# Second token half loaded into the tile of its low part, and a larger planned price for a transfer on SyncE

## The chip, the cores and the metric

The kernel runs on one core of a Trainium2 chip. Time is the device time of one execution in microseconds (us). Besides the plain runs there is one profiled execution, whose trace gives the start and the end of every instruction. The engines are named as in the profile: PE (TensorE matmul; PEld is its weight load), DVE (VectorE), ACT (ScalarE), POOL (GpSimd), SP (SyncE, which here only issues DMA transfers; its queue is "SPq").

## The reference

One decoder layer on x of 1024 tokens by 2048 channels, all in float32:

```python
h = rmsnorm(x, ln_g)
proj = h @ w_in                       # 2048 -> 6672 columns
g_u, g_v, g_z, d_q, d_k, d_v, d_z, d_a, d_b, c_q, c_z = split(proj)
out_a = gmlp_spatial_gating(g_u, g_v, ...) * silu(g_z)      # 4 groups of 128, chunks of 128 tokens
q, k, v = heads(causal_conv_silu(concat(d_q, d_k, d_v)))    # 8 heads of 128
o = gated_delta_rule(l2norm(q), l2norm(k), v, g, beta)      # chunks of 64: a 64x64 triangular
out_b = rmsnorm(o, dn_norm_g) * silu(d_z)                   # solve, then a scan of the state
out_c = cross_attention(c_q, mem) * silu(c_z)               # 4 heads, 256 memory tokens
y = rmsnorm(x + concat(out_a, out_b, out_c) @ w_out, final_g)
```

## The kernel before, in words

**Products.** A float32 product is made of three matmuls on parts: `split_to(hi, lo, src, eng)` (line 422) lets ACT copy `src`, rounded, into `hi` (in the profile a CAST), and DVE subtract, `lo = src - hi` (a TENSOR_TENSOR). A triple on PE is then hi·hi + lo·hi + hi·lo, each 128x128 by 128x512, accumulated in a PSUM bank `acc`. `ahi[k]`, `alo[k]` are the parts of the normalised tokens, transposed: 16 tiles k of 128 channels by 512 tokens. `whi`, `wlo` are the parts of the weights.

**Two token halves.** The 1024 tokens go in two halves of 512. `ahi`/`alo` hold one half at a time, 128x512 float32 per k (256 KB). While the first half is projected, the second one is normalised and its 16 transposed tiles are written to DRAM, `hT_d`, as are those of the first, `h0_d`. When the first half is done, `refill(k)` (lines 1218 to 1223) brings tile k of the second half from `hT_d[k]` into `ahi[k]`, `alo[k]`, with k running inside the first product that uses it: `project([column(0, 0), column(1, 0)], before)` (line 1232) makes two columns of 128 at once, for each k first `refill(k)`, then a small matmul for the decays, then two triples (6 large matmuls).

**The raw ring.** `wraw` (lines 372 to 380) is a ring of four slots of 128x512. Weight pieces are loaded into it (`raw_piece`, line 426) and split from there into `whi`, `wlo`. In the kernel before, `refill` takes its slots from the same ring. The ring hands its slots out in the order of the program's text, so a load waits until the slot's previous content has been split.

**What follows a refill.** Gated DeltaNet for pairs of heads: `front` (columns, convolution), `inverted` (the triangular inverse: 31 dependent steps of small DVE operations), `values`, and `back` with `scan_step` (PE products `dn<-...`; `vs`, `states`, `steps` are its tiles). `left_sums(j)` (line 725) runs beside it: it loads four tiles (`hTd`, `h0d`) into `zg`, forms sums and differences and stores them to `s_d`; these serve a later, Strassen-like stage that works on both halves at once (loads `raws<-sd`, `y<-sd`, to about 1440 us), before the output product and the final norm. `vd` and `od` in DRAM keep what the scans hand on.

**What sets the order.** Nothing is issued as the text stands. Every operation is recorded as an `Op`, and `Plan.issue` (lines 218 to 277) sorts them all with a small model of the chip: each engine is free at some time, each operation has a `cost` (and a transfer also a data time at `DMA_RATE` 300 bytes/ns and a fixed 1600 ns), a result is seen on another engine some 35 to 78 ns later, PE gets 600 ns more (`SLACK`). The engine that can go first takes the ready operation of the lowest rank (`with rank(n)`); the list, sorted by the planned time, is then emitted, and line 277, `o.fn(*o.args, **o.kw)`, is the line of every instruction in the profile. `Plan.price` (line 180) sets the costs; for a `dma_start` on SP it is 380 ns before. Per engine the emitted order is fixed; the chip runs it with waits on semaphores, so SP issues its transfers strictly in that order, and one whose tile isn't free yet holds all behind it.

Of the kernel before, what the change touches and what calls it, by code (L numbers as in the profile page):

```python
# [9 lines left out]
F32 = mybir.dt.float32  # L10
# [52 lines left out]
class Plan:  # L63
# [21 lines left out]
    @contextmanager  # L85
    def rank(self, cls):
        old, self.cls = self.cls, cls
        yield
        self.cls = old
# [91 lines left out]
    def price(self, o, name, outs, ins):  # L181

        out = outs[0]
        n = math.prod(out.shape[1:])
        both = [*outs, *ins]
        psum = any(i.space == PSUM for i in both)
        pointer = any(i.shape[-1] == 1 and math.prod(i.shape[1:]) == 1 for i in ins[1:])
        o.nbytes = o.lock = 0
        o.lat = 0.0
        if name == "dma_start":  # L190
            o.cost = {"sp": 380.0, "act": 100.0, "pool": 800.0}[o.eng]
            rows = math.prod(out.shape[:-1])
            o.nbytes = max(4 * math.prod(out.shape), 512 * rows)
            src = ins[0]
            pieces = src.shape[-1] < 128 or out.shape[-1] < 128
            if out.space == DRAM:
                o.lat = 3000.0
            elif pieces or out.shape[0] < 32:
                o.lat = 2400.0
            elif list(src.ap)[0][0] == 0:  # L200
                o.lat = 4000.0
        elif o.eng == "pe":
            passes = 1 if ins[0].dtype == F32R else 2 if name == "transpose" else 4
            o.cost = max(13.3 + n / 2.4 * passes, 222.0 if passes == 4 else 110.0) if out.shape[0] == P else 30.0
            o.lat = 175.0
        elif o.eng == "act":
            o.cost = (165.0 if psum else 200.0) + 0.82 * n + (105.0 if pointer else 0.0)
            o.cost += 190.0 if "accum_out" in o.kw else 0.0
        elif o.eng == "dve":
            n = max([n] + [math.prod(i.shape[1:]) for i in ins])  # L210
            o.cost = (n + 151) / 0.96 + (60.0 if pointer and name == "scalar_tensor_tensor" else 0.0)
            o.lock = not psum and (name.startswith("tensor_") or name == "scalar_tensor_tensor")
            o.lock = o.lock and name != "tensor_reduce"
        else:
            o.lock = 1
            if name in ("memset", "affine_select"):
                o.cost = 100.0 + 0.83 * n * (1 if name == "memset" else 1.4)
                o.lat = 800.0 if name == "affine_select" else 0.0
            else:
                o.cost = 750.0 + 150.0 * (n - 1) if n < 8 else 200.0 + 2.1 * n  # L220
# [60 lines left out]
def kernel(  # L281
# [29 lines left out]
    V, S, G, PE, Q = R.dve, R.act, R.pool, R.pe, R.sp  # L311
# [5 lines left out]
    def DT(shape, name, dt=F32):  # L317
        return dr.tile(list(shape), dt, name=name, tag=name)[:]
# [41 lines left out]
    def tok(ap):  # L360

        return ap.rearrange("p (t c) -> p t c", c=P)
# [7 lines left out]
    ahi = [ahq[k // 4][:, :, k % 4] for k in range(KT)]  # L370
    alo = [alq[k // 4][:, :, k % 4] for k in range(KT)]
    wraw = Ring("wraw", 2, [P, 2 * HT])
# [33 lines left out]
    hT_d = DT([KT, P, HT], "hTd")  # L406
# [15 lines left out]
    def split_to(hi, lo, src, eng):  # L422
        S.copy(hi, src)
        eng.tensor_tensor(out=lo, in0=src, in1=hi, op=ALU.subtract)
# [145 lines left out]
    for k in range(KT):  # L570
# [5 lines left out]
        with rank(2):  # L576
            for sl in kv_parts(k):
                raw = kvraw[k % 4][:, sl]
# [638 lines left out]

    def refill(k):

        raw = wraw()  # L1220
        with rank(2):
            Q.dma_start(raw, hT_d[k])
            split_to(ahi[k], alo[k], tok(raw), V)

    a = tpb()

    def before(k):
        refill(k)
        decay_mm(a, k)
# [555 lines left out]
```

## Time and profile before

| | before |
|---|---|
| median of 3 runs | 1644.65 us (1640.99 to 1645.63) |
| profiled execution | 1644.06 us, span 1642.3 us |
| PE busy | 1615.6 us (98%), 8570 matmuls |
| DVE busy | 1317.5 us (80%) |
| ACT busy | 1023.9 us (62%) |
| mean DMA rate | 255 GB/s, 419.51 MB |
| granted PE clock | 0.996 |

The busy rows say how long an engine worked anywhere in the span. For an engine that is 98% busy the question is where the other 2% are, and that is read from the time line and from the waits, not from the shares.

### The profile page before, as it was taken

How to read it: one execution, taken by the hardware profiler on the slowest of the kernel's cores; microseconds unless marked ns; L12 is line 12 of the kernel's file. 1: busy time of each engine (PE TensorE's matmuls, PEld its weight loads, DVE VectorE, ACT ScalarE, POOL GpSimd, SP SyncE). 2: the span in 40 equal slices, each digit the busy share in tenths (PEclk: the TensorE clock that was granted, in tenths of full speed). 3: DMA queues.
4: the chain of work that ended last, by engine and by line, in shares of the span. 5: the costliest groups of instructions: out<-in, count | busy, mean ns of one | idle time of the engine just before them, and what ended most of it. 6: DMA issues, size and time to landing. Idle time of an engine off the chain costs nothing.

```text
span 1642.3 us, 26178 instructions
## 1 busy us (share of the span) xinstructions
PE 1615.6 (98%) x8570; PEld 1354.3 (82%) x8570; DVE 1317.5 (80%) x2288; ACT 1023.9 (62%) x2235; POOL 109.8 (7%) x139
## 2 busy tenths in 40 slices
PE   8999999999999999999999999999999999999997
PEld 6888887878788888888888887888888888888886
DVE  4866796847879869899998997788768897688875
ACT  6957674665855457976776446766666774344445
POOL 0001100120210001100101000000000000000001
PEclk9999999999999999999999999999999999999999
DMA  8889887885886867689878986878968769678646
GB/s 266 255 229 283 256 272 209 249 266 177 278 290 221 267 219 254 207 276 323 298 243 263 304 240 188 297 253 300 313 218 286 260 231 353 202 264 304 219 142 242
DMA packets 316659, 419.51 MB, mean 255 GB/s; under 512 B 57773, under 2 KB 138342, under 8 KB 316522
## 3 DMA queue, kind: packets, MB, share of 16 engines
q1 hardware_dynamic: 314818, 414.67, 77.6%
q0 software_dynamic: 1088, 2.10, 0.4%
q8 instruction: 67, 1.10, 0.3%
q10 hardware_dynamic: 616, 1.07, 0.2%
q14 instruction: 70, 0.57, 0.1%
HBM read 334.33 MB, written 82.87 MB: 254 GB/s over the span
## 4 chain that ended last, share of the span: by engine, by line
PE 89%; DMA 4%; DVE 3%; ACT 1%; issue 1%; SPq 1%; POOLq 0%; POOL 0%; DVEq 0%; ACTq 0%
PE acc L277 68%; PE dn L277 21%; DMA raws<-sd 1%; DMA wraw<-in_w_in_dram 1%; SPq L277 1%; DVE alo L277 1%; DVE wlo L277 0%; DMA od<-vs 0%; DVE y L277 0%; DMA zg<-h0d 0%; ACT whi L277 0%; DMA wraw<-in_w_out_dram 0%; DMA h0d<-tn 0%; DMA el<-vd 0%; DMA y<-in_w_out_dram 0%
## 5 line engine op out<-in xcount | busy, mean ns | idle before, releaser
L277 PE MATMUL acc<-ahi,whi 128*128 128x512 f32 (+1 forms) x1152 | 450.8, 392 | 4.1 <-ACT whi L277 2.1
L277 PE MATMUL acc<-alo,whi 128*128 128x512 f32 (+1 forms) x1152 | 451.7, 392 | 0.2 <-DVE alo L277 0.2
L277 PE MATMUL acc<-ahi,wlo 128*128 128x512 f32 (+1 forms) x1152 | 450.2, 391 | 0.4 <-DVE small L277 0.4
L277 PEld LDWEIGHTS acc<-ahi,whi 128*128 128x128 f32 x1152 | 216.9, 188 | 46.4 <-ACT whi L277 2.7
L277 PEld LDWEIGHTS acc<-ahi,wlo 128*128 128x128 f32 x1152 | 217.0, 188 | 41.7 <-DVE wlo L277 0.6
L277 PEld LDWEIGHTS acc<-alo,whi 128*128 128x128 f32 x1152 | 217.0, 188 | 41.2 <-DVE alo L277 0.9
L277 PE MATMUL acc<-ahi,zh 128*128 128x512 f32 x736 | 233.0, 393 | 0.0
L277 ACT CAST whi<-wraw 128x512 fp32r<-128x512 f32 (+1 forms) x170 | 137.1, 808 | 113.1 <-PE acc L277 73.2
L277 DVE TENSOR_TENSOR alo<-raws,ahi 128x1024 fp32r<-128x1024 f32 x131 | 159.8, 1221 | 39.8 <-ACT ahi L277 38.8
L277 ACT CAST ahi<-raws 128x1024 fp32r<-128x1024 f32 x131 | 137.4, 1049 | 68.8 <-PE dn L277 28.1
L277 DVE TENSOR_TENSOR wlo<-wraw,whi 128x1024 fp32r<-128x1024 f32 (+1 forms) x138 | 135.1, 980 | 49.0 <-ACT whi L277 39.2
L277 PEld LDWEIGHTS acc<-ahi,zh 128*128 128x128 f32 x736 | 137.0, 188 | 26.9
L277 PE MATMUL acc<-ahi,zl 128*128 128x512 f32 x368 | 145.0, 394 | 0.0
L277 DVE TENSOR_TENSOR ahi<-y,ahi 128x1024 fp32r<-128x1024 f32 x65 | 79.4, 1222 | 18.6 <-ACT ahi L277 18.3
L277 ACT CAST ahi<-y 128x1024 fp32r<-128x1024 f32 x65 | 68.3, 1051 | 35.0 <-PE acc L277 18.6
L277 PEld LDWEIGHTS acc<-ahi,zl 128*128 128x128 f32 x368 | 69.3, 188 | 13.4
L277 ACT CAST zh<-wraw 128x1024 fp32r<-128x1024 f32 x36 | 37.8, 1051 | 51.8 <-issue 23.2
L277 POOL TENSOR_TENSOR small<-small,mhalf 128x1 f32<-128x1 f32 x26 | 17.9, 692 | 626.9 <-DVE small L277 626.9
L277 PE MATMUL dn<-wlo,ahi 128*128 128x512 f32 x152 | 59.0, 389 | 0.0
L277 PE MATMUL dn<-whi,alo 128*128 128x512 f32 x152 | 59.0, 389 | 0.0
L277 POOL TENSOR_TENSOR hs<-hs,mhalf 128x4 f32<-128x4 f32 x32 | 46.7, 1460 | 182.7 <-DVE hs L277 181.7
L277 PE MATMUL dn<-whi,ahi 128*128 128x512 f32 x152 | 58.8, 389 | 0.0
(408 smaller groups left out, 3205.3 us busy)
## 6 DMA issues: line engine op xcount, KB each, us to landing
wraw<-in_w_in_dram SPq DMA_DIRECT2D x268, 256.0 KB
raws<-sd SPq DMA_DIRECT2D x148, 256.0 KB
y<-in_w_in_dram SPq DMA_DIRECT2D x92, 256.0 KB
y<-sd SPq DMA_DIRECT2D x77, 256.0 KB
wraw<-in_w_out_dram SPq DMA_DIRECT2D x64, 256.0 KB
raws<-h0d SPq DMA_DIRECT2D x54, 256.0 KB
y<-in_w_out_dram SPq DMA_DIRECT2D x33, 256.0 KB
low<-wlo SPq DMA_DIRECT2D x32, 256.0 KB
```

Source lines behind the costliest of these rows:

```text
L277: o.fn(*o.args, **o.kw)
```

## The change

Two edits. `Plan.price` prices a transfer issued on SP at 490 ns instead of 380 ns. And `refill(k)` no longer takes a slot of `wraw`: it loads `hT_d[k]` into `alo[k]` itself, seen as plain float32, in the tile's own layout (`tok` turns the 128x512 source into 128x4x128; a row of `alo[k]` is four pieces of 128 floats that lie 4x128 floats apart); the split then reads that tile, writes `ahi[k]`, and subtracts in place, `alo[k] = alo[k] - ahi[k]`.

```diff
@@ -188,7 +188,7 @@
         if name == "dma_start":
-            o.cost = {"sp": 380.0, "act": 100.0, "pool": 800.0}[o.eng]
+            o.cost = {"sp": 490.0, "act": 100.0, "pool": 800.0}[o.eng]
@@ -1217,10 +1217,10 @@
     def refill(k):
 
-        raw = wraw()
+        raw = alo[k].bitcast(F32)
         with rank(2):
-            Q.dma_start(raw, hT_d[k])
-            split_to(ahi[k], alo[k], tok(raw), V)
+            Q.dma_start(raw, tok(hT_d[k]))
+            split_to(ahi[k], alo[k], raw, V)
```

Both edits change what the planner counts with, and so the emitted order. On PE the first 461 of 6733 rows of the order (equal neighbours make one row) and the last 853 are the same before and after; on SP, of 1456 rows, the first 64 and the last 62. In between, rows stand earlier or later by a few to some tens of places. Three places follow, of SP and of PE (in a row: operation, out<-in with the number of each tile's allocation, shape).

**SP at the refills, before:** the last 11 of the 16 loads `wraw<-hTd` lie between weight pieces (`in_w_in_dram`), all in the same ring.

```order
L277 DMA wraw1_72<-hTd_114 128x512
L277 DMA wraw0_71<-hTd_114 128x512
L277 DMA wraw0_71<-in_w_in_dram 128x4x128
L277 DMA zg0_81<-h0d_113 128x512
L277 DMA wraw1_72<-hTd_114 128x512 x2
L277 DMA wraw0_71<-in_w_in_dram 128x4x128
L277 DMA wraw0_71<-hTd_114 128x512
L277 DMA wraw1_72<-in_w_in_dram 128x4x128 x2
L277 DMA wraw0_71<-hTd_114 128x512 x2
L277 DMA wraw1_72<-hTd_114 128x512 x2
L277 DMA wraw0_71<-hTd_114 128x512
L277 DMA wraw0_71<-in_w_in_dram 128x4x128
```

**SP at the refills, after:** tiles 5 to 15, into `alo1` to `alo3` (each name is a block of four k).

```order
L277 DMA alo1_68<-hTd_114 128x4x128
L277 DMA wraw0_71<-in_w_in_dram 128x4x128
L277 DMA alo1_68<-hTd_114 128x4x128 x2
L277 DMA sd0_1_3_307<-zg0_81 128x512
L277 DMA alo1_68<-hTd_114 128x4x128
L277 DMA alo2_69<-hTd_114 128x4x128
L277 DMA zg0_81<-h0d_113 128x512
L277 DMA alo2_69<-hTd_114 128x4x128 x3
L277 DMA alo3_70<-hTd_114 128x4x128 x3
L277 DMA wraw1_72<-in_w_in_dram 128x4x128
L277 DMA alo3_70<-hTd_114 128x4x128
L277 DMA wraw1_72<-in_w_in_dram 128x4x128
```

Between the fifth and the last refill there stood four weight pieces, now there are two; the others went behind, and the last refill load is eight rows earlier in SP's order.

**SP at a left sum, before:** `gt` is filled for the next inverse; behind it stand `E`, a low part, and then the two `zg` loads of `left_sums`.

```order
L277 DMA gt_6_452<-gt_6_452 64x4x64
L277 DMA E0_83<-gcd1_371 128x4x128
L277 DMA wlo0_75<-low2944_2_420 128x512
L277 DMA zg1_82<-hTd_114 128x512
L277 DMA wraw1_72<-in_w_in_dram 128x4x128
L277 DMA zg0_81<-h0d_113 128x512
L277 DMA wlo1_76<-low2944_3_421 128x512
```

**After:**

```order
L277 DMA gt_6_452<-gt_6_452 64x4x64
L277 DMA zg1_82<-hTd_114 128x512
L277 DMA zg0_81<-h0d_113 128x512
L277 DMA wlo1_76<-low2944_3_421 128x512
L277 DMA wraw1_72<-in_w_in_dram 128x4x128
L277 DMA E0_83<-gcd1_371 128x4x128
L277 DMA wlo1_76<-low3840_0_443 128x512
```

The two `zg` loads follow `gt` directly. On PE, in the same place, **before** one large matmul of the next column stands ahead of the four `steps` products of the scan and six behind them, up to `dn<-states,kT`:

```order
L277 MATMUL acc0_105<-ahi0_63,whi4_77 128x512
L277 MATMUL dn0_109<-steps_367,kd_6_407 128x128
L277 MATMUL dn1_110<-steps_367,kd_7_422 128x128
L277 MATMUL dn0_109<-steps_367,ai_6_411 128x128
L277 MATMUL dn1_110<-steps_367,ai_7_426 128x128
L277 MATMUL acc0_105<-alo0_67,whi4_77 128x512
```

**after** 13 of them stand ahead:

```order
L277 MATMUL acc0_105<-alo0_67,whi4_77 128x512
L277 MATMUL acc0_105<-ahi0_63,wlo4_78 128x512
L277 MATMUL acc0_105<-ahi1_64,whi0_73 128x512
L277 MATMUL dn0_109<-steps_367,kd_6_407 128x128
L277 MATMUL dn1_110<-steps_367,kd_7_422 128x128
L277 MATMUL dn0_109<-steps_367,ai_6_411 128x128
L277 MATMUL dn1_110<-steps_367,ai_7_426 128x128
L277 MATMUL acc0_105<-alo1_68,whi0_73 128x512
```

so that the scan's products stand 12 large matmuls later in the column's run.

**SP at `el`, before:** a tile that PE reads for the late scan comes behind four stores `vd`, a `gt`, two loads and a load `xd`.

```order
L277 DMA vd1_0_264<-E1_84 128x128
L277 DMA vd1_1_265<-E1_84 128x128
L277 DMA vd1_2_266<-E1_84 128x128
L277 DMA vd1_3_267<-E1_84 128x128
L277 DMA gt_15_627<-gt_15_627 64x4x64
L277 DMA raws_498<-sd0_4_3_319 128x512
L277 DMA raws_498<-sd0_5_3_323 128x512
L277 DMA xd00_0_244<-y2_501 128x512
L277 DMA el0_517<-vd0_2_262 128x512
L277 DMA xd00_1_245<-y2_501 128x512
L277 DMA tn3_88<-vd0_3_263 128x512
```

**After:** `xd00_0` and `el0` stand ahead of the four `vd`; the second pair, `xd00_1` and `tn3`, still behind them.

```order
L277 DMA xd00_0_244<-y2_501 128x512
L277 DMA el0_517<-vd0_2_262 128x512
L277 DMA vd1_0_264<-E1_84 128x128
L277 DMA vd1_1_265<-E1_84 128x128
L277 DMA vd1_2_266<-E1_84 128x128
L277 DMA vd1_3_267<-E1_84 128x128
L277 DMA xd00_1_245<-y2_501 128x512
L277 DMA tn3_88<-vd0_3_263 128x512
```

Elsewhere: the stores `od0_2<-vs`, `od0_3<-vs` of a scan, which before stood right behind four loads `raws<-h0d`, stand after the change behind ten more transfers (`y3` twice two, `raws` four, `wraw1` two).

## The prediction

> **What bounds the kernel now.** I read the page first, for who is busy and what ends last.
>
> ```profile
> span 1642.3 us, 26178 instructions
> PE 1615.6 (98%) x8570; PEld 1354.3 (82%) x8570; DVE 1317.5 (80%) x2288; ACT 1023.9 (62%) x2235; POOL 109.8 (7%) x139
> PE 89%; DMA 4%; DVE 3%; ACT 1%; issue 1%; SPq 1%; POOLq 0%; POOL 0%; DVEq 0%; ACTq 0%
> ```
>
> PE bounds it, and the change gives PE nothing less to do: the count of matmuls stays. So the time can only move by PE's idle time, 1642.3 - 1615.6 = 26.7 us in all. The second view, busy time in stretches that I cut at the stages, says where that idle time lies (columns: stretch, its length, then busy us and count of PE, PEld, DVE, ACT, POOL, then the granted PE clock, DMA share, GB/s).
>
> ```profile
> 0.00:72.00 72.00, 64.69 (x394) 54.95 (x395) 45.86 (x73) 55.93 (x109) 5.02 (x18) 1.00 0.85 268
> ...
> 206.00:262.00 56.00, 53.77 (x246) 43.33 (x245) 51.53 (x124) 35.55 (x94) 1.08 (x1) 1.00 0.84 260
> 262.00:410.00 148.00, 144.97 (x915) 123.09 (x914) 99.59 (x266) 90.66 (x274) 21.16 (x19) 0.99 0.75 224
> 410.00:1000.00 590.00, 587.22 (x3026) 490.07 (x3024) 526.15 (x876) 380.65 (x781) 48.41 (x57) 1.00 0.79 260
> 1000.00:1020.00 20.00, 17.28 (x115) 14.41 (x115) 13.88 (x23) 13.71 (x32) 1.54 (x3) 0.91 0.85 276
> ...
> 1440.00:1642.30 202.30, 193.99 (x856) 160.28 (x854) 153.87 (x220) 96.35 (x146) 4.81 (x8) 0.99 0.70 234
> ```
>
> Length less PE busy: 7.3 us in the head and 8.3 us in the tail, where PE's order is the same before and after. Left for the change: 2.2 (the refill stage), 3.0, 2.8, 2.7, and 0.3 in the two stretches not shown: 11.0 us. That is a hard floor of 1644.06 - 11.0 = 1633 for the profiled execution, unless the head or tail moves. The third view, PE's waits grouped by what ended them (us in total, times, longest), names the large pieces.
>
> ```profile
> PE dn L277 <- ACT vs L277: 3.0, 1, 3.0
> PE dn L277 <- DMA el<-vd: 2.1, 1, 2.1
> PE acc L277 <- ACT whi L277: 2.1, 2, 1.5
> ```
>
> Single waits at single places: a matter of what stands in which queue when. That is what both edits touch.
>
> **The change, part by part.** *Refill, direct.* Counts stay: 16 loads of 256 KB, 16 casts, 16 subtractions. What moves is what a load waits for: no longer a slot of the raw ring but PE's last read of alo[k]. When is that, and when is tile k needed? From PE's time line, with SP's and ACT's at the end of the stage:
>
> ```profile
> 216.95 0.39 PE L277 MATMUL acc<-alo,whi 128*128 128x512 f32 x1
> ...
> 228.09 0.39 PE L277 MATMUL acc<-ahi,whi 128*128 128x512 f32 x1
> ...
> 246.68 0.39 PE L277 MATMUL acc<-ahi,wlo 128*128 128x512 f32 x1
> 247.95 0.73 PE L277 MATMUL acc<-ahi,whi 128*128 128x512 f32 x2 [0.89 <-ACT ahi L277]
> 248.92 0.50 PE L277 MATMUL acc<-alo,whi 128*128 128x512 f32 x1 [0.24 <-DVE alo L277]
> ...
> 252.44 0.39 PE L277 MATMUL acc<-ahi,wlo 128*128 128x512 f32 x1
> 253.93 0.50 PE L277 MATMUL acc<-ahi,whi 128*128 128x512 f32 x1 [1.10 <-ACT xr L277]
> ```
>
> ```profile
> 239.65 5.14 SPq L277 DMA_DIRECT2D wraw<-hTd  x5
> ```
>
> ```profile
> 246.54 1.36 ACT L277 CAST ahi<-wraw 128x512 fp32r<-128x512 f32 x2 [0.82 <-DMA wraw<-hTd]
> ...
> 252.04 0.62 ACT L277 CAST whi<-wraw 128x512 fp32r<-128x512 f32 x1 [1.20 <-DMA wraw<-in_w_in_dram]
> ```
>
> The pitch of large matmuls comes from a row of the chain of waits:
>
> ```profile
> 1394.63 65.28 PE acc L277 x288
> ```
>
> 65.28 / 288 = 0.227 us. The last product of the first half reads alo[0] at 216.95 and alo[k] some 0.68 k later (three matmuls per k); the pair product needs tile k at 228.09 + 1.36 k (six). So tile 0 has 228.1 - 217.3 = 10.8 us from free to needed, tile 15 21 us. In that time: issue 0.4, landing 4 to 6 (by the 5.66 and 4.74 us of single 256 KB transfers below), cast 0.62, subtraction 0.7 (a 128x512 one of DVE, below): under 8 us. Before, the last five loads were issued only at 239.65 to 244.8, because the ring was full of pieces not yet split, and the last cast ended at 247.9, past its need of 228.09 + 15 x 1.36 = 248.5 once the split is added. PE lost, start to start beyond the pitch: 247.95 - 246.68 - 0.23 = 1.04; some 0.4 at 248.92; and 253.93 - 252.44 - 0.23 = 1.26, where ACT's xr copies came late behind a weight cast that waited 1.20 us for its piece, which SP had issued behind the refills. In SP's new order all refills stand ahead of the last weight pieces, and those no longer share slots with them. I take all of it: **-2.7**; bounds 0 (the subtractions alternate with the inverse on DVE, 51.53 of 56 us busy, so they may stay late) and -2.7.
>
> What the direct load costs: its rows in the tile are 512-byte pieces instead of 2 KB. The fastest and the slowest 50 us of the trace (the slow one writes and loads mostly in such pieces):
>
> ```profile
> 100.00:150.00 50.00, 50.00 (x253) 41.72 (x252) 33.45 (x74) 35.77 (x100) 5.21 (x7) 1.00 0.81 228
> 1350.00:1400.00 50.00, 50.00 (x224) 41.32 (x223) 41.23 (x55) 22.93 (x35) 0.00 (x0) 1.00 0.93 335
> ```
>
> 228 / 0.81 = 281 and 335 / 0.93 = 360 GB/s of a full share. The 4.19 MB take 14.9 instead of 11.6 us of all engines: 3.3 us at most, in a stage of 56 us with the engines at 84%, of which the free 16% are 9 us. I take 0; bound +3.3, when the transfers end last. [...]
>
> *Dearer issue.* 490 for 380 changes only what the planner believes: transfers on SP seem later, and SP's loads and their users are put elsewhere. A real run of four loads without a wait (1.74 us, among the rivals' rows) has a pitch of 0.435, so the new number is not clearly nearer. Two of the 11 us are hit by it in a way that the order shows.
>
> *Place 2, the 3.0 us wait:*
>
> ```profile
> 366.70 0.40 PE L277 MATMUL acc<-ahi,whi 128*128 128x512 f32 x1
> 370.13 0.60 PE L277 MATMUL dn<-states,kT 128*128 128x128 f32 x3 [3.03 <-ACT vs L277]
> ```
>
> ```profile
> 358.54 0.62 SPq L277 DMA_DIRECT2D gt<-gt  x1
> ...
> 362.48 1.01 SPq L277 DMA_DIRECT2D zg<-h0d  x1
> ```
>
> ```profile
> 362.48 5.66 DMA zg<-h0d
> ...
> 368.16 0.70 DVE zg L277
> ```
>
> DVE stood behind a left sum whose load landed at 368.14, with the scan's `states` behind it, so ACT's `vs` and PE were late. After, that load stands two places behind gt: issued about 359.7, 2.8 us earlier. And PE reaches the scan's product 12 large matmuls later, 12 x 0.227 = 2.7 us. 2.8 + 2.7 covers 3.2 (370.13 - 366.70 - 0.23). I take **-3.0**, bounds -3.2 and 0.
>
> *Place 3, the 2.1 us wait:*
>
> ```profile
> 1016.14 0.68 PE L277 MATMUL dn<-wsT,el 128*128 128x128 f32 x2 [2.15 <-DMA el<-vd]
> ```
>
> ```profile
> 1011.36 4.74 DMA el<-vd
> ```
>
> ```profile
> 1006.82 0.69 DVE L277 TENSOR_TENSOR y<-y,el 128x512 f32<-128x512 f32 x1
> ```
>
> el is free at 1007.5 but loaded at 1011.36, behind four stores, gt and two loads. After, it stands ahead of these: up to 3.5 us sooner, more than the loss of 2.6 (start to start). But the tn3 load, still behind the stores, has its reader 9 matmuls (2 us) later and may wait in its place. I take **-1.5**, bounds -2.6 and 0.
>
> *New waits.* Some 5400 PE rows between the common ends stand in a new order, against the same DVE and SP. The old order had, beside the three places, 11.0 - 2.2 - 3.0 - 2.1 = 3.7 us of waits that no one aimed at; the new one will have its own, in part the same. I take **+2.2** beyond the old ones, bounds 0 and +7 (two more of the size of place 2).
>
> Sum: -2.7 - 3.0 - 1.5 + 2.2 = -5.0 on the profiled 1644.06, which is 0.6 below the median of the runs: **1639**.
>
> **The rivals.**
> *All gains, nothing new:* -2.7 - 3.2 - 2.6, and 1.5 of the small old waits: 1644.06 - 10 = 1634. For it speaks that each place is relieved by more than it lost; against it, that 5400 rows seldom come out without a new wait.
> *Waits only move:* place 2 and 3 come back elsewhere at their size, or the refill's subtractions stay late behind the inverse: 1644. For it: DVE is 526.15 of 590 us busy from 410 to 1000, so a relieved queue meets the next.
> *Short pieces bound the refill:* the 2.7 don't come and 3.3 are added: 1639 + 6 = 1645. Against it: the needed rate is one tile per 1.36 us, 193 GB/s, with 281 in the slowest window.
> *Slower: ACT held at a scan slot.*
>
> ```profile
> 403.89 6.15 DMA od<-vs
> ```
>
> ```profile
> 411.66 0.62 ACT L277 ACTIVATE vs<-E 128x512 f32<-128x512 f32 x1
> ```
>
> ```profile
> 401.57 1.74 SPq L277 DMA_DIRECT2D raws<-h0d  x4
> ...
> 412.57 2.58 SPq L277 DMA_DIRECT2D wraw<-in_w_in_dram  x3
> ```
>
> That `vs` overwrites the tile that the od store reads. After, the store stands behind ten more transfers, the last of them issued about 413.4, so it would land at 413.4 + 6.15 = 419.6. If ACT came to `vs` at its old 411.66, it would be held 8.0 us with the casts for PE behind it. Before PE goes on, a cast and its subtraction follow, by the page's groups (busy us, mean ns of one):
>
> ```profile
> L277 DVE TENSOR_TENSOR alo<-raws,ahi 128x1024 fp32r<-128x1024 f32 x131 | 159.8, 1221 | 39.8 <-ACT ahi L277 38.8
> L277 ACT CAST ahi<-raws 128x1024 fp32r<-128x1024 f32 x131 | 137.4, 1049 | 68.8 <-PE dn L277 28.1
> ```
>
> 1.05 + 1.22; and with the scan that late place 3 keeps its 1.5: 1639.1 + 8.0 + 2.3 + 1.5 = 1651. Against it: ACT's new order puts some eight operations of up to 1.05 us ahead of `vs`, so it arrives near 420. The kernel is slower than can be missed from a hold of 6.7 us on, an arrival before 413; later arrivals cost less.
> *Nothing happens:* the order shows moves in the middle, so this is the second rival's 1644.
>
> **How the numbers follow.** Forecast 0.48, own range 1634 to 1642; all gains 0.14; waits only move 0.16; short pieces 0.05; slower 0.17. A measurement of this kernel tells about 0.3% from no change, 4.9 us: below 1639.7 is faster, above 1649.6 slower. The forecast lies on that edge; of its 0.48 I count 0.33 as faster, 0.15 as the same. Faster 0.33 + 0.14 = 0.47; the same 0.15 + 0.16 + 0.05 = 0.36; slower 0.17. The range of 8 in 10, 1633.5 to 1648, holds the forecast, the middle cases, most of the best one, and little of the slow one.
>
> **What the new profile would show.** Refill: the loads alo<-hTd issued between 217 and 230, PE without idle from 240 to 256; wrong, if a PE wait for alo or ahi stands there. Place 2: no PE wait above 0.5 us near 370; wrong, if `vs` still shows. Place 3: el issued near 1008, and either no wait or one for tn. New waits: PE's waits in the middle sum to 4 to 7 us. If PE's busy time itself moved by more than 1 us, or head or tail by more than 0.5, the sum was made on the wrong ground. If ACT idles several us before `vs` near 412, the slow case has come.

## The result, and the profile after

| | before | changed |
|---|---|---|
| median, 6 runs each | 1645.14 us | 1636.26 us (1633.78 to 1639.75) |
| ratio | | 0.9950, interval 0.9932 to 0.9967 |
| the same pair again, beside the experiments | 1645.64 us (25 runs) | 1637.62 us (6 runs), 0.9944, 0.9929 to 0.9960 |
| profiled execution | 1644.06 us, span 1642.3 | 1639.64 us, span 1637.9; again: 1638.04, span 1636.3 |

The change makes the kernel 8 to 9 us faster, 0.5 to 0.6%; 1639 (1633.5 to 1648) had been forecast. The page of the changed kernel, first lines and the shares of the chain of waits:

```profile
span 1637.9 us, 26168 instructions
...
PE 1613.4 (99%) x8570; PEld 1351.3 (83%) x8570; DVE 1320.6 (81%) x2288; ACT 1024.3 (63%) x2235; POOL 126.2 (8%) x139
...
PE 90%; DMA 4%; DVE 4%; issue 1%; ACT 0%; SPq 0%; POOLq 0%; POOL 0%; DVEq 0%; ACTq 0%
```

As many matmuls as before, but PE's busy time is 2.2 us lower (1615.6 before). The prediction had said that only PE's idle time can move; the reason is below. In the profiled executions the change is smaller than in the medians: the span fell by 4.4 us, 2.2 of them idle time, and in the second profile by 6.0, 4.6 of them idle time. Idle time by the same stretches as before (columns as in the prediction):

```profile
206.00:262.00 56.00, 55.60 (x253) 45.77 (x252) 51.17 (x120) 33.10 (x83) 4.37 (x1) 1.00 0.87 260
262.00:410.00 148.00, 147.74 (x932) 125.04 (x932) 104.81 (x272) 96.37 (x284) 18.93 (x19) 1.00 0.78 236
410.00:1000.00 590.00, 584.40 (x3002) 486.75 (x3000) 520.85 (x864) 375.43 (x769) 62.90 (x58) 1.00 0.78 255
1000.00:1020.00 20.00, 18.53 (x98) 15.27 (x98) 15.45 (x24) 12.50 (x22) 1.34 (x1) 1.00 0.84 271
1020.00:1440.00 420.00, 419.39 (x2356) 353.75 (x2356) 338.10 (x528) 261.63 (x569) 13.46 (x18) 1.00 0.81 271
```

The refill stage: 0.4 us idle for 2.2 before; the stretch of place 2: 0.3 for 3.0; place 3: 1.5 for 2.7. From 410 to 1000 it is 5.6 for 2.8: new waits. PE's waits by what ended them, and where the largest stand (PE's time line):

```profile
PE dn L277 <- DVE ai L277: 5.6, 2, 3.4
...
PE dn L277 <- DMA el<-vd: 0.9, 1, 0.9
...
PE dn L277 <- ACT vs L277: 0.2, 1, 0.2
```

```profile
687.27 0.39 PE L277 MATMUL dn<-inv 128*128 128x256 f32 x1 [2.20 <-DVE ai L277]
...
726.89 0.39 PE L277 MATMUL dn<-inv 128*128 128x256 f32 x1 [3.40 <-DVE ai L277]
```

The three old waits have nearly gone and two new ones, for DVE in the triangular inverse, have come.

The tiles of the refill, loads on SP, casts on ACT and subtractions on DVE (duration in ns, shortest, median, longest; first and last start):

```profile
L277 SPq DMA_DIRECT2D alo<-hTd x16: 518/600/2188, 216.6 to 233.4; - x16
L277 ACT CAST ahi<-alo x16: 607/622/642, 220.6 to 239.8; 128x512 fp32r<-128x512 f32 x16
L277 DVE TENSOR_TENSOR alo<-alo,ahi x16: 671/673/693, 221.3 to 243.3; 128x512 fp32r<-128x512 f32 x16
```

The last load is issued at 233.4 (before: 244.5) and the last tile is split at 244.0 (before 248.9). By PE's time line the pair product began at 227.8 in this run, so tile 15 was needed at 227.8 + 20.4 = 248.2: 4 us of margin.

### The profile page after: what moved, and what is told of

It reads as the page before. It is cut to its first block, busy times and chain, and to the rows that moved or that the text cites. A ratio compares the mean times of both kernels' runs of the same rounds, so it can differ in the third digit from the quotient of the medians.

```text
span 1637.9 us, 26168 instructions
## 1 busy us (share of the span) xinstructions
PE 1613.4 (99%) x8570; PEld 1351.3 (83%) x8570; DVE 1320.6 (81%) x2288; ACT 1024.3 (63%) x2235; POOL 126.2 (8%) x139
## 2 busy tenths in 40 slices
DMA packets 322803, 419.51 MB, mean 256 GB/s; under 512 B 57773, under 2 KB 146534, under 8 KB 322666
## 4 chain that ended last, share of the span: by engine, by line
PE 90%; DMA 4%; DVE 4%; issue 1%; ACT 0%; SPq 0%; POOLq 0%; POOL 0%; DVEq 0%; ACTq 0%
PE acc L277 69%; PE dn L277 21%; DMA y<-in_w_in_dram 1%; DMA wraw<-in_w_in_dram 1%; DVE wlo L277 1%; DVE y L277 1%; DVE alo L277 1%; DMA qT<-in_mem_dram 0%; DMA mixd<-qT 0%; SPq L277 0%; DVE tn L277 0%; DMA inv<-gdr 0%; DMA h0d<-tn 0%; DMA xr<-pd 0%; DMA kT<-in_mem_dram 0%
## 5 line engine op out<-in xcount | busy, mean ns | idle before, releaser
L277 PE MATMUL acc<-ahi,zh 128*128 128x512 f32 x736 | 233.4, 394 | 0.0
L277 POOL TENSOR_TENSOR small<-small,mhalf 128x1 f32<-128x1 f32 x26 | 24.2, 931 | 592.2 <-DVE small L277 592.2
```

## The experiments

Two theories stood against each other at first. A, the prediction's: each part of the change relieves its own place. B: any edit redraws the whole order, and the sum of the waits is a draw. Others came up on the way.

### The two edits apart, and a price between

e1 is the changed kernel again. e2 has the direct refill alone:

```diff
-        raw = wraw()
+        raw = alo[k].bitcast(F32)
         with rank(2):
-            Q.dma_start(raw, hT_d[k])
-            split_to(ahi[k], alo[k], tok(raw), V)
+            Q.dma_start(raw, tok(hT_d[k]))
+            split_to(ahi[k], alo[k], raw, V)
```

e3 has the price alone, e4 the direct refill with 435:

```diff
-            o.cost = {"sp": 380.0, "act": 100.0, "pool": 800.0}[o.eng]
+            o.cost = {"sp": 490.0, "act": 100.0, "pool": 800.0}[o.eng]
```

> The changed kernel once more, beside the others, with a second profile. Both theories expect the time on record, 1634 to 1640 us, 0.5% below the kernel before. What it is for: the first profile of it shows two waits of PE for DVE (2.2 and 3.4 us, near 685 and 723 us). If they belong to the order, they stand there again, within 0.5 us; if they are chance of that execution (it took 1639.6 us, the median of the six is 1636.3), one or both are shorter by over 1 us and this execution is shorter by as much.

> The direct refill alone; a transfer on SyncE is planned at 380 ns as before. Theory A (each part does its own): PE's three waits of the refill stage (1.04, 0.4 and 1.26 us beyond the pitch, near 247 to 254 us) are gone, under 0.5 us are left there; the zg loads of the left sum still stand three to five places behind gt, and el behind the four vd stores, so that the waits near 370 (3.2 us) and 1014 (2.3 us) stay at over 1.5 us each. Time 1644.65 - 2.7 = 1642, give or take 2 for new waits elsewhere. Theory B (the order as a whole is redrawn by any edit, and the sum of the waits is a draw): PE's waits sit at other places altogether, and the time may be anything from 1634 to 1648.

> The price of 490 ns alone; the refill goes through the raw ring as before. Theory A: the waits of the refill stage stay (over 1.5 us in all between 240 and 256 us); the zg loads stand right behind gt and el ahead of the second four vd stores, so the waits near 370 and 1014 us are under 1 us each: 1644.65 - 2.8 - 1.3 = 1640.5, give or take 2. Theory B: as above, anything from 1634 to 1648, with the refill stage changed too.

> The direct refill with a price of 435 ns, the pitch of SyncE that a run of four loads without a wait shows. Theory A: the zg loads and el stand as early as at 490, so all three places are relieved: within 3 us of the changed kernel, 1634 to 1640. Theory B (490 is one draw among many): 435 redraws the order behind 400 us and the time differs from the changed kernel by over 3 us to either side. A third theory, that the gain grows with how dear SyncE is planned, would put it half way, near 1640.5.

Measured, against 1645.64 for the kernel before: e1 1637.62; e2 **1653.03**, ratio 1.0041 (1.0025 to 1.0057), slower; e3 1638.87, 0.9962 (0.9949 to 0.9976); e4 1640.41, 0.9965 (0.9952 to 0.9979).

In e1 the wait near 685 us was 0.3 us instead of 2.2, and that near 723 stood at 2.0 instead of 3.4: both shorter by over 1 us, and the execution 1.6 us shorter. The place belongs to the order, the size in part to the execution. e4 is 2.8 us above e1, at the edge of what theory A allows and where the third theory, half way, put it.

e2 did what theory A says at the refill, but its time is 11 us above the 1642 of that theory: it lost elsewhere. Its stretch of the refill, and PE's waits:

```profile
206.00:262.00 56.00, 55.62 (x257) 45.80 (x256) 50.44 (x124) 37.16 (x102) 1.03 (x1) 1.00 0.92 267
```

```profile
PE acc L277 <- ACT xr L277: 4.5, 2, 4.1
PE dn L277 <- DMA el<-vd: 4.1, 2, 3.8
PE dn L277 <- ACT vs L277: 3.1, 1, 3.1
PE dn L277 <- DVE ai L277: 2.3, 1, 2.3
```

0.4 us idle at the refill, where 2.2 stood; but `vs` (place 2) still 3.1, `el` (place 3) now 3.8, and a new wait of 4.1 for ACT near 401. A gain at its place, and a loss of 7.4 in all. (This profile is the longest of the eight runs of e2, 4 us above their median.)

e3, the price alone, has the gain, and its refill stage is clean too, though the loads still go through the ring:

```profile
206.00:262.00 56.00, 55.97 (x254) 45.63 (x253) 52.82 (x122) 34.78 (x86) 4.37 (x1) 1.00 0.85 262
```

Theory A had the waits of this stage stay. The loads through the ring still go out until 244.1, and the last tile is split at 249.2, no earlier than in the kernel before (244.5 and 248.9); PE has no wait there in its new order. So the ring was not what cost the 2.7 us; the order around it was. Theory A holds for where waits sit, not for which edit pays. Between e3 and e1 the 1.3 us are not clear of noise (the intervals of the ratios overlap), so at 490 no worth of the direct refill is shown.

### The order of before, with three places of SyncE moved by hand

e5 keeps every engine's old order and moves seven transfers on SP after the sort:

```diff
         self.ops.sort(key=lambda o: (o.at, o.idx))
+        # SP only: zg1<-hTd, zg0<-h0d of the left sum to right behind gt_6<-gt_6;
+        #          vd1_0..3<-E1 and gt_15<-gt_15 to right behind el0<-vd0_2
+        for move in self.MOVES:
+            self.move(*move)
```

> The kernel before with its own order on every engine, but for seven transfers of SyncE: the two zg loads of the left sum moved right behind gt (two and three places earlier), and the four vd stores and one gt moved behind el (el five places earlier). Nothing else moves, PE's order above all. By the prediction's chains, place 2 (3.2 us near 367) shrinks by what the load comes earlier, 2.8 less a wait of it for its slot, to under 1.2 us, and place 3 (2.3 us near 1014) by 2.5, to under 0.5; the time falls by 3.5 to 5 us to 1640.5 to 1642. If place 2 went only because PE comes 12 matmuls later in the changed kernel, it stays over 2 us here and the time falls by 2 us or less. If PE's waits only move on, the two places are relieved but the time is within 1.5 us of the kernel before.

Measured: 1639.34 against 1646.74, ratio 0.9953 (0.9936 to 0.9970): 7.4 us from seven transfers, as much as the whole change gave, and more than the 5 expected at most. PE's time line at place 2, before and in e5 (line 302 is line 277 there):

```profile
365.09 0.61 PE L277 MATMUL dn<-steps,ai 128*128 128x128 f32 x4
...
375.48 0.61 PE L277 MATMUL dn<-steps,kd 128*128 128x128 f32 x4
```

```profile
365.48 0.61 PE L302 MATMUL dn<-steps,ai 128*128 128x128 f32 x4
...
370.97 0.61 PE L302 MATMUL dn<-steps,kd 128*128 128x128 f32 x4
...
375.38 0.96 PE L302 MATMUL dn<-states,kT 128*128 128x128 f32 x3 [1.28 <-ACT vs L302]
```

The same run of PE's instructions takes 370.97 - 365.48 = 5.49 us instead of 10.39: 4.9 us less, where the wait was 3.03. Of that a new wait of 1.3 comes back one step of the scan later. At place 3 no wait for `el` is left, and the same PE instructions, from the 32 small `dn<-tblk,gt` to the next `acc<-ahi,zh` behind the `dn<-y,ut`, take 3.5 us (1010.24 to 1013.70) instead of 7.3 (1013.30 to 1020.61): 3.9 us less, where the wait was 2.15. The two gains less the new wait, 4.9 + 3.9 - 1.3 = 7.5, are the 7.4 measured. SP's order alone was the cause of places 2 and 3, PE's later product was not needed; and each of these two waits cost more than its length. The granted clock shows why.

### What a wait costs beyond its length

The kernel before, places 2 and 3, busy time in short stretches (the number behind POOL's is the granted PE clock):

```profile
366.00:370.00 4.00, 1.09 (x5) 0.56 (x3) 1.78 (x4) 0.19 (x1) 0.00 (x0) 1.00 1.07 338
370.00:372.00 2.00, 1.87 (x9) 1.60 (x10) 0.61 (x2) 0.57 (x4) 0.00 (x0) 0.80 1.01 251
372.00:374.00 2.00, 2.00 (x8) 1.79 (x7) 1.03 (x5) 1.00 (x3) 0.00 (x0) 0.50 0.93 284
374.00:376.00 2.00, 2.00 (x11) 1.65 (x10) 0.00 (x0) 0.17 (x1) 0.00 (x0) 0.85 0.95 271
376.00:378.00 2.00, 2.00 (x15) 1.79 (x15) 1.40 (x6) 0.89 (x5) 0.00 (x0) 1.00 0.08 24
...
1016.00:1018.00 2.00, 1.85 (x9) 1.86 (x10) 0.00 (x0) 0.00 (x0) 0.00 (x0) 0.58 1.05 378
1018.00:1020.00 2.00, 2.00 (x12) 1.74 (x11) 0.73 (x3) 0.83 (x4) 0.00 (x0) 0.57 0.47 153
```

The clock falls to half after PE is back at work (at 370.13 and 1016.14). In the matmuls themselves, e1 behind its wait of 2.02 us at 724:

```profile
724.13 0.39 PE L277 MATMUL dn<-inv 128*128 128x256 f32 x1 [2.02 <-DVE ai L277]
...
725.42 0.63 PE L277 MATMUL acc<-ahi,wlo 128*128 128x512 f32 x1
725.85 0.63 PE L277 MATMUL acc<-ahi,whi 128*128 128x512 f32 x1
...
728.41 0.58 PE L277 MATMUL acc<-ahi,whi 128*128 128x512 f32 x1
728.82 0.39 PE L277 MATMUL acc<-alo,whi 128*128 128x512 f32 x1
```

From 725.42 to 728.82 there are eight matmuls in 3.4 us, a pitch of 0.425 for 0.227: 8 x 0.2 = 1.6 us lost on top of the wait. With 3.2 + 1.6 = 4.8 for place 2 the 4.9 of e5 is met. This also explains most of the fall of PE's busy time in the changed kernel: half-speed matmuls count as busy (2.00 of the 2 us from 372 to 374, at a clock of 0.50). Behind the head the kernel before has two such stretches, the changed kernel has one, behind its new wait at 726.89 (e1 too, above): one fewer, 1.6 of the 2.2 us. The loss was not the same behind every wait, though. In e2 the clock fell before PE was back at 405.40 from the wait for `xr`, and stayed at half until about 411, twice as long:

```profile
401.00:405.00 4.00, 0.31 (x2) 0.00 (x0) 2.39 (x8) 3.94 (x16) 2.83 (x2) 0.88 0.00 0
405.00:407.00 2.00, 1.60 (x4) 1.31 (x5) 2.00 (x5) 2.00 (x5) 0.00 (x0) 0.50 0.00 0
407.00:409.00 2.00, 2.00 (x7) 1.52 (x6) 2.00 (x5) 0.76 (x3) 0.00 (x0) 0.50 0.00 0
409.00:411.00 2.00, 2.00 (x7) 1.51 (x6) 2.00 (x5) 0.00 (x0) 0.00 (x0) 0.52 0.00 0
```

### The price

e6, e7 and e8 are the changed kernel with other prices:

```diff
-            o.cost = {"sp": 490.0, "act": 100.0, "pool": 800.0}[o.eng]
+            o.cost = {"sp": 300.0, "act": 100.0, "pool": 800.0}[o.eng]   # e6; e7: 560.0; e8: 650.0
```

> The direct refill with a transfer on SyncE planned at 300 ns, under the 320 that the shortest takes. Theory D (a plan that has SyncE too fast puts PE's work ahead of its data): slower than at 380 alone, 1653 or more, with PE's waits between 200 and 1440 us summing to over 20 us. Theory B (each price is a draw): anywhere between 1636 and 1655.

> The direct refill at 560 ns, dearer than a 128x512 transfer without a wait (0.435) and near the 600 that a direct refill load takes. Theory D: no more data comes late, so as fast as at 490, 1635 to 1640. Theory B: anywhere between 1636 and 1655. A third theory, that 490 is about the true price and a dearer one costs as a cheaper one does: 1641 to 1646.

> The same at 650 ns. Theory D: 1635 to 1641, or a little slower where the planner now holds PE back for transfers that are there. Theory B: anywhere. Third theory: slower than at 560, 1643 to 1650.

Measured against 1646.74: e6 1656.03 (1.0054, 1.0039 to 1.0069); e7 **1632.20** (0.9905, 0.9887 to 0.9923); e8 **1668.14** (1.0128, 1.0113 to 1.0144). From 380 to 560 dearer is better with the direct refill, as theory D has it (between 300 and 380, and between 435 and 490, the steps are within the noise), and then the kernel is 36 us slower. No theory had both: D put e7 at 1635 to 1640 and e8 near it, B put e7 at 1636 or more, the third put e7 at 1641 or more and e8 at 1650 at most. In e6 the time is as D had it, but PE's waits from 200 to 1440 us sum to some 17 us, not to over 20. The waits of e7 and of e8:

```profile
PE dn L277 <- DMA kT<-in_mem_dram: 4.9, 1, 4.9
PE acc L277 <- ACT whi L277: 1.8, 2, 1.3
PE dn L277 <- DVE ut L277: 1.4, 1, 1.4
```

```profile
PE acc L277 <- ACT zh L277: 8.7, 2, 5.3
PE dn L277 <- ACT jk L277: 5.1, 1, 5.1
```

e7 has no wait over 1.6 us outside the head (the 4.9 stands at its very start; the kernel before, the changed kernel and e10 have 4.7, 4.8 and 5.0 there).

That led to a new theory, P. `Plan.issue` computes a time for every operation, and so its own end of the program (the planned start of the last operation). Written out for each kernel, beside the measured median:

| price, ns | refill | plan's end | measured | measured - plan |
|---|---|---|---|---|
| 300 | direct | 1631.5 | 1656.0 | 24.5 |
| 380 | ring (before) | 1625.3 | 1645.6 | 20.3 |
| 380 | direct (e2) | 1628.1 | 1653.0 | 24.9 |
| 435 | direct (e4) | 1625.6 | 1640.4 | 14.8 |
| 490 | ring (e3) | 1623.5 | 1638.9 | 15.4 |
| 490 | direct (the change) | 1621.8 | 1637.6 | 15.8 |
| 560 | direct (e7) | 1621.7 | 1632.2 | 10.5 |
| 650 | direct (e8) | 1658.0 | 1668.1 | 10.1 |

The last column, what the plan did not foresee, falls as the price rises, though not at every step, and at 380 it differs by 4.6 between the two refills. It is a net figure: waits that are in no plan, planned gaps that come out shorter, and the half clock. The plan's own end goes up and down without any pattern. And the plan knows of waits itself: its gaps of PE over 0.8 us behind the head are, for the kernel before, 1.3 at 246.9, 1.2 at 252.7 and 1.7 at 406.1, which are the two large waits of the refill stage and the one near 411; for the changed kernel none; for e2 a gap of 5.3 at 390.8, which is its new wait of 4.1 near 401; for e8 8.4 at 416.7 and 3.8 at 426.0, where the chip waited 5.1 and 3.4. Places 2 and 3 are not in the plan of the kernel before. To test P: at 570 the plan ends 30.7 us later than at 560, with gaps of 9.6 at 895.5 and 6.4 at 991.9; at 590 it ends early again.

> The direct refill at 570 ns, 10 ns over the price that gave 1632.2 us. Theory P (measured time = the end that Plan.issue itself computes for its list + what the plan leaves out, and this remainder falls as the price gets honest): the plan ends at 1621.7 us at 560 and at 1652.4 at 570, and the remainders so far are 24.5 at 300, 25.0 at 380, 14.8 at 435, 15.8 at 490, 10.5 at 560, 10.1 at 650. So 1652.4 + 10.3 = 1663, give or take 4. Theory D (only the price counts, and dearer is better up to a cliff between 560 and 650): 1632 to 1640.

> The direct refill at 590 ns. Theory P: the plan ends at 1622.4, so 1622.4 + 10.3 = 1633, give or take 4, although 570 is slow. Theory D: a price beyond the cliff, so slower than at 570.

> 560 ns with the refill through the raw ring as before. Theory P: the plan ends at 1626.9, 5.2 us later than with the direct refill, so 1626.9 + 10.5 = 1637, give or take 4. If the direct refill has a worth of its own that shows at an honest price, the refill stage (206 to 262 us) has over 1.5 us more of PE's idle time than at 560 with the direct refill; if not, under 0.7, and the difference lies elsewhere.

Measured against 1644.91: e9 **1663.78** (1.0108, 1.0088 to 1.0128); e10 **1633.55** (0.9924, 0.9905 to 0.9943); e11 1636.03 (0.9933, 0.9911 to 0.9956). Forecast were 1663, 1633 and 1637. Theory D falls, P stands; the remainders are 11.4, 11.2 and 9.1, so beyond 560 they fall no further. The longest wait of e9 is where its plan had put the gap:

```profile
909.90 0.69 PE L277 MATMUL dn<-ident,gt 128*128 128x128 f32 x2 [8.68 <-ACT et L277]
```

The profiled execution of e11 took 4198 us, where the other four took 1632 to 1637, so the second half of its expectation, whether the direct refill shows at its own place at 560, stays open.

### The refill alone, with the two places mended

e12 is e2 with the same moves on SP as e5 at places 2 and 3.

> The direct refill alone at 380 ns (1653 us), with its own order but for the same two places of SyncE moved by hand: the two zg loads right behind gt, the four vd stores and gt behind el. If the loss of the refill alone is the order of SyncE at these places, with the clock that PE loses after long waits, the waits for vs (3.1) and el (4.1) fall to under 1.5 in all, and the time by 6 to 9 us to 1644 to 1647; the wait of 4.1 for ACT's xr near 401 us stays. If it is the refill itself, the time stays within 3 us of 1653.

Measured: 1646.98 (1.0005, 0.9994 to 1.0016 of the kernel before), 6 us below e2. PE's wait at place 2 and the groups:

```profile
380.53 1.07 PE L302 MATMUL dn<-states,kT 128*128 128x128 f32 x4 [0.42 <-ACT vs L302]
```

```profile
PE acc L302 <- ACT xr L302: 5.2, 2, 4.2
...
PE dn L302 <- DMA el<-vd: 2.0, 2, 1.4
```

`vs` fell from 3.1 to 0.4, `el` from 4.1 to 2.0 (more than expected is left), and the 4.2 for `xr`, planned, stays. The time is what the first case of the expectation has, but it doesn't show what that case says. The two places stood in the kernel before as well, and there the same moves gave 7.4 (e5). With the places mended on both sides the refill alone is still slower, 1646.98 against 1639.34 of e5 (ratios 1.0005 and 0.9953 to the kernel before), by 7.6 us, as much as without the moves. So the order of SP at these places is not where the refill alone loses. What e2 and e12 have, and the kernel before and e5 have not, is the wait of over 4 us for `xr` and the slow matmuls behind it:

```profile
399.38 0.80 PE L302 MATMUL acc<-ahi,whi 128*128 128x512 f32 x1 [4.23 <-ACT xr L302]
...
404.67 1.19 PE L302 MATMUL dn<-ident,vs 128*128 128x128 f32 x8
```

From 399.38 to 404.67 PE makes 12 large matmuls in 5.3 us, which at the pitch of 0.227 take 2.7. The wait and this loss, 4.2 + 2.6 = 6.8, are most of the 7.6, and the wait is the gap of 5.3 in the plan of e2. No run takes this wait away, so that it is the cause is likely but not tested. The refill's own stage is not slow (0.4 us idle in e2).

## Why the prediction came out as it did

The direction, the place of the old waits and the range were right; the forecast (-5.0 on the profiled execution) was short of the -8 to -9 of the medians. On the profiled executions -4.4 and -6.0 came out, near the forecast, but that is in part luck. Counted as idle time plus 1.6 us for each half-clock stretch, in the first profile place 2 gave 2.7 + 1.6 and place 3 gave 1.2 + 1.6, together 7.1 us instead of 4.5; the refill gave 1.8 instead of 2.7; and the new waits from 410 to 1000 us took 2.8 + 1.6 = 4.4 instead of 2.2. These errors nearly cancel. Why the medians moved by more than the profiles, no profile shows; the profile of the kernel before is 1.1 us below the median of its six runs, the first of the changed kernel 3.4 above. By the prediction's own steps:

- **"PE has nothing less to do, so only idle time moves": wrong ground, the step that failed.** Its own test, busy time moving by over 1 us, came out at -2.2 (-1.4 in e1). The sum put what PE loses behind a long wait at nothing; it was 1.6 us for each half-clock stretch of 3.4 us. So place 2, put at 3.0 and 3.2 at most, was worth 4.9 in e5, and place 3, put at 1.5 and 2.6 at most, 3.9. The same term belongs to the new waits: the changed kernel has one such stretch of its own.
- **The refill, -2.7: the size nearly right, the cause wrong.** The waits for `ahi`, `alo` and `xr` are gone, and one of 0.4 for `tn` stands there. The last tile was ready 4 us ahead of its need. But the price alone emptied the stage too, and the two large waits stood in the old plan: the plan knew that it had no room there. "All of it" was not the direct load's doing, and the load's edit alone made the kernel slower.
- **The direct load at no cost: right.** From the first issue to the first cast it took 220.6 - 216.6 = 4.0 us. What was not counted is its issue, 0.6 us for 0.32, 4.5 us of SP's time for 16. ACT's casts waited 3.0 us in all for the loads, PE for none of the refill's tiles. The stage moved 260 GB/s in both kernels, with the DMA engines busy for 87% of it instead of 84%: by an estimate 0.03 x 56 = 1.7 us more of their time, where the bound had 3.3.
- **Place 2: right in mechanism.** The `zg` load came earlier and `vs` waits 0.2 us. Of the two causes given, SP's order alone does it (e5).
- **Place 3: right, and only half gone.** el was issued at 1007.6, as said ("near 1008"), no wait for tn came, but one of 0.9 for el stayed (1.5 in e1).
- **New waits, +2.2: put too low.** The two waits for the inverse are 5.6 in the first profile and 2.3 in the second; with their half clock 7.2 and 3.9, where the bounds were 0 and 7. PE's idle time from 72 to 1440 us sums to 8.3 and 6.3, where 4 to 7 had been named (11.0 before). The old wait near 411 (1.7), kept in the sum among the unaimed ones, went as well.
- **"490 changes only what the planner believes ... not clearly nearer": too little.** What it believes decides how much of the plan comes true. The remainder over the plan fell from 20.3 to 15.8 and the plan's end from 1625.3 to 1621.8. With 490, the -8.0 of e1 is 3.5 from the plan and 4.5 from the remainder.
- **The slower rival (ACT held at `vs` near 412):** the last of the ten transfers that stand ahead of the od stores was issued at about 404, not at 413.4, so the stores were issued at 404.4, and ACT ran `vs` at 413.5 without a wait. The mechanism never came up. That the refill edit alone is slower by 7.4 was in no rival, nor that the price alone gives the gain (e3).

The version that beats both is the change with 560 instead of 490: 1632.20, ratio 0.9905 to the kernel before, where the change had 0.9944 and 0.9950.

## What to carry to other kernels

Where a list planner sets the order, read its own end and its own gaps first: the large gaps of a plan came back on the chip at their places, if not at their size, and a measured time splits into the plan's end and a remainder, which here shrank as the price rose to 560 and then stayed near 10. Judge a cost by the remainder over several values, never by one time: 560, 570 and 590 gave 1632, 1664 and 1634 us here, and the plan's end with the remainder of 10.3 foretold the second and the third within 1 us. Look behind a wait of PE before it is counted at its length: here four waits of 2.0 to 3.4 us had a half-clock stretch of 3.4 us behind them, by an estimate 1.6 us more each, and one of 2.2 had none. And before a repair is taken as the cure of a loss, make the same repair in the kernel that it is compared with: e12 alone seemed to cure the refill, e12 beside e5 did not.

## What the runs showed of the hardware

**The clock after a wait.** PE ran at half clock for about 3.4 us behind waits of 3.03 us (place 2), 2.15 us (place 3) and 2.02 us (e1 at 724). Around the end of the wait of 4.1 us in e2 it was about 7 us. The length of the wait alone does not tell whether the clock falls: in the changed kernel the wait of 2.20 us before 687.27 left the clock whole, the one of 3.40 before 726.89 did not:

```profile
687.20:689.20 2.00, 1.93 (x11) 1.74 (x12) 2.00 (x5) 2.00 (x5) 0.23 (x1) 1.00 0.86 251
689.20:691.20 2.00, 2.00 (x10) 1.62 (x10) 2.00 (x2) 2.00 (x7) 0.00 (x0) 1.00 0.49 184
```

```profile
727.00:729.00 2.00, 2.00 (x10) 1.71 (x10) 2.00 (x3) 0.62 (x1) 0.00 (x0) 0.67 1.00 357
729.00:731.00 2.00, 2.00 (x6) 1.61 (x5) 2.00 (x4) 0.63 (x1) 0.00 (x0) 0.50 0.81 213
```

What decides it, no run here shows.

**Issue on SyncE.** A 256 KB load into a tile as 512-byte pieces held SP for 0.60 us (changed kernel), into whole 2 KB rows for 0.32 (kernel before; medians of 16 each). The changed kernel moves 322803 packets, the kernel before 316659: 384 more for each of the 16 loads, four packets in place of one for each of its 128 rows.
